# Attention and index heads taken in pairs, with the score products of two heads issued alternately

## The chip, the cores and the metric

The kernel runs on one core of one Trainium2 chip, as one program and one launch. The metric is device time in microseconds. The core's engines work side by side: TensorE (PE) multiplies matrices, VectorE (DVE) and ScalarE (ACT) work elementwise, SyncE (SP) issues the loads from HBM. Matrix products land in PSUM, which this kernel uses as 8 banks of 128 partitions x 2 KB.

## The reference

The reference is a network of three layers for one sequence of 256 tokens with 1024 features, in float32. Each layer takes a normalised and modulated input, mixes tokens, and has a feed-forward part. What matters here are the three mixing parts, in which every head has 64 features:

- First layer: 8 heads with a relative-position bias, beside a pooling branch and gates.
- Even layer: 8 heads with forget gates (a bias from cumulative sums), then 8 sliding-window heads with a sink and 2 shared key/value heads.
- Odd layer: 8 index heads score all pairs of tokens (`logits = einsum('bqhd,bsd->bqhs', iqi, ik)`, relu, weighted sum over heads); for each token the 64 best are kept; then 16 heads attend to those, with 4 shared key/value heads.

Each attention head computes softmax(q k^T + bias) v. The last feed-forward part is a mixture of 8 experts.

## The kernel before

Activations are kept as features x tokens, so a head's q and k are 64 partitions x 256 tokens. Two heads share a tile: one lies on partitions 0 to 63, the other on 64 to 127. The 256 query tokens are two blocks of 128, and the mask is causal, so a head's scores are a 128 x 128 product (first block) and a 128 x 256 product (second block), 384 columns in one PSUM bank. The products with weights (`mm3`, L212) are made in three passes of split float32r numbers; score products, transposes and value products are float32, which the chip runs as two passes each where an LDWEIGHTS and a MATMUL stand for one pass.

`attend` (L570) is a generator with five stages, one for each turn: (1) the two score products (`scores`, L562); (2) on DVE the sum with the bias and the row minimum (L580; scores are kept negated), on ACT the exponential with its row sum (L585), plus the sink's small steps in the sliding-window heads; (3) on DVE the reciprocal and the scaling (L595, L597); (4) on PE three transposes (L601), copied out of PSUM by ACT (L603); (5) for the second head of a pair, the value products of both heads, alternately, on the two halves of the output partitions (L610), and `after`, which splits the result into two float32r parts (L648, L649).

`weave` (L614) runs these generators. A turn advances every running head by one stage, oldest first, then starts one new head if its inputs are there, then does one step of a "piece": a quarter of a projection (`gemm_t_steps`, 12 matmul passes) or of an output product (`acc_steps`, 12 passes). So in steady state a head starts in each turn. A piece may wait for a number of finished heads: an output product needs its four heads. In the odd layer `weave` runs twice: first the 8 index heads (`index_head`, L1076: scores, then relu on ACT and weighted sums on DVE) and the selection (`select`, L1090, a chain of maxima and replacements on DVE), with three projections; then the 16 heads with two projections and three output products.

Two things set the order of work. The order of ACT's instructions is the order of the code (`ORDER = {'main': 'a', ...}`). The order on PE and DVE is planned by the framework from the data dependencies and its own estimate of times; it may, for example, put a score product between two transposes. Tiles come from rings: 8 PSUM banks for everything, 4 probability tiles (`N_PROB`), 3 transposed ones (`N_PROBT`), 2 bias tiles in the forget-gate heads, 8 small ones. While output products run, four banks hold their sums and one the sum of squares for the next norm (`acc_begin`, `norm_begin`).

Weights stream through `Stream` (L71): SP loads 5 tiles ahead, ACT and DVE split each into two parts (L195, L198), in the weaves by halves.

Of the kernel before, what the change touches and what calls it, by code (L numbers as in the profile page):

```python
# [152 lines left out]
class Kernel:  # L153
# [84 lines left out]
    def gemm_t_steps(self, key, h, kt, n=256, fine=False):  # L238
        """[n columns of w on partitions (two tiles a bank), tokens]"""
# [17 lines left out]
    def gemm_t2(self, keys, h):  # L257
        """Blocks of 256 columns, a row of h at a time as it is made"""
# [10 lines left out]
    def flush(self):  # L269
        """Work put off so that the tensor engine needn't wait for it"""  # L270
# [7 lines left out]
    def gemm_n_steps(self, key, h, fine=False):  # L278
        """[tokens on partitions (two tiles), 256 columns of w]"""
# [15 lines left out]
    def gemm_narrow(self, hi, lo, h):  # L295
        """[8 columns of w on partitions, tokens]"""
# [18 lines left out]
    def ada_step(self, layer, g, kt, raw, defer, weigh):  # L315
        """128 rows of a group of modulations' weights. weigh: on the vector engine, summed over the rows later"""
# [41 lines left out]
    def ada_turn(self, a):  # L358
        """The sums, on every 32nd partition, go to a column for each 128 of them"""
# [14 lines left out]
    def ada_finish(self, upto=None):  # L374
        """One step of what is left to do for the oldest group, or all that a group needs"""
# [19 lines left out]
    def rstd(self, ps, shape, first=None):  # L395
        """-2 / root of a mean square; the gains make up for the -2. first: a factor that goes ahead, in place"""
# [22 lines left out]
    def norm_begin(self, gain, layer=None, scale_i=None):  # L419
        """The norm that follows the coming updates of x"""  # L420
# [23 lines left out]
    def norm_first(self):  # L444
        """The first norm: the modulation is the last to come"""
# [89 lines left out]
    def acc_end(self, key, act, gate, n_ada):  # L535
        """The last rows: each feature tile goes on into the stream and its norm"""
# [33 lines left out]
    def attend(self, q, k, v, add, pair, sink=None, after=None):  # L570
        """One head, a stage at a time; a pair's second one ends both"""
        nc = self.nc
        ps = self.scores(self.psum(), q, k)
        if callable(add):
            add = add()
        yield
        p = self.sp.tile([128, 384], F32, name="prob", bufs=N_PROB)
        mn, sm = self.tiny(), self.tiny()
        for t, c in self.HALVES:
            nc.vector.tensor_tensor_reduce(out=p[:, c], in0=ps[:, c], in1=add[t], op0=OP.add, op1=OP.min,  # L580
                                           scale=1.0, scalar=3e38, accum_out=mn[:, t:t + 1])
        if sink is not None:
            nc.vector.tensor_scalar(mn, mn, sink, None, op0=OP.min)
        for t, c in self.HALVES:
            nc.scalar.activation(p[:, c], p[:, c], AF.Exp, bias=mn[:, t:t + 1], scale=-1.0,  # L585
                                 accum_out=sm[:, t:t + 1])
        if sink is not None:
            e = self.tiny()
            nc.vector.tensor_scalar(e, mn, sink, None, op0=OP.subtract)
            nc.scalar.activation(e, e, AF.Exp)  # L590
        yield
        if sink is not None:
            nc.vector.tensor_tensor(sm, sm, e, op=OP.add)
        ri = self.tiny()
        nc.vector.reciprocal(ri, sm)  # L595
        for t, c in self.HALVES:
            nc.vector.tensor_scalar(p[:, c], p[:, c], ri[:, t:t + 1], None, op0=OP.mult)  # L597
# [8 lines left out]
        if after:  # L606
            ps = self.psum()
            for t, (c, w) in enumerate(((0, 256), (128, 128))):
                for s, (vs, ps_t) in enumerate(pair):
                    nc.tensor.matmul(ps[64 * s:64 * s + 64, 0, c:c + w], vs[t], ps_t[:, 256 * t:256 * t + w],  # L610
                                     start=t == 0, stop=t == 1, skip_group_check=True)
            after(ps)

    def weave(self, heads, pieces):  # L614
        """Heads in a pipeline of stages, with the steps of other work between.
        heads: (pieces that have to be done, stages); pieces: (heads that have to be done, steps)"""
        running, h, p, done, piece = [], 0, 0, 0, None
        while h < len(heads) or p < len(pieces) or running:
            for g in list(running):
# [3 lines left out]
            if h < len(heads) and p >= heads[h][0]:  # L623
# [10 lines left out]
    def pair_out(self):  # L634
        """Where two heads' results meet, and their split for the product that follows"""
        nc = self.nc
        res, pairs = ([], []), {}

        def pair(j):
            return pairs.setdefault(j, [])  # L640
# [10 lines left out]
        return res, pair, after  # L651

# [128 lines left out]
    def layer1(self):  # L781
# [75 lines left out]
        att, pair, after = self.pair_out()  # L857
        heads = []
        for hd in range(8):
            def mk(hd=hd):  # L860
                j, s = hd // 2, hd % 2
                b = slice(64 * s, 64 * s + 64)
                bias = self.bias[j]
                return self.attend(qk[j // 2][b, j % 2], qk[2 + j // 2][b, j % 2],
                                   [vn[hd // 4][:, t, (hd % 4) * 64:(hd % 4) * 64 + 64] for t in range(2)],
                                   (bias[:, s, 128:256], bias[:, s, :]), pair(j), after=after(j) if s else None)
            heads.append((0 if hd < 4 else 4, mk))
# [72 lines left out]
    def even(self):  # L940
# [6 lines left out]
        # forget gates  # L947
# [53 lines left out]
        att, pair, after = self.pair_out()  # L1001
# [18 lines left out]
        for hd in range(8):  # L1020
            def mk(hd=hd):
                j, s = hd // 2, hd % 2
                b = slice(64 * s, 64 * s + 64)
                return self.attend(fq[j // 2][b, j % 2], fk[j // 2][b, j % 2],
                                   [fv[hd // 4][:, t, (hd % 4) * 64:(hd % 4) * 64 + 64] for t in range(2)],
                                   fox_bias(hd), pair(j), after=after(j) if s else None)
            heads.append((1 if hd < 4 else 3, mk))
        for j in range(4):
            for s in range(2):
                def mk(j=j, s=s):  # L1030
                    b = slice(64 * s, 64 * s + 64)
                    return self.attend(sq[j // 2][b, j % 2], self.sk[b, 0],
# [667 lines left out]
```

## Time and profile before

| what | value |
|---|---|
| median of 3 runs (lowest, highest) | 1365.48 us (1364.51, 1366.25) |
| span of the profiled execution | 1360.7 us |
| mean granted PE clock | 0.986 |
| TensorE busy | 1311.9 us (96%) |
| VectorE busy | 970.2 us (71%) |
| ScalarE busy | 737.6 us (54%) |
| DMA | 342.8 MB, mean 252 GB/s |

The span runs from the first to the last instruction on the core; the time of a run also holds what lies before and after. Busy times overlap between engines. Successive matmuls overlap in PE's pipeline, so the duration of one (0.28 us for a 256-column pass) is longer than the distance between two starts (0.12 us); prices on PE are read from starts. In a timeline, "x4" merges four neighbouring instructions of the same line, and fp32 products show two records each. Heads are at work from 63 to 111 us (first layer), 474 to 553 (even layer) and 810 to 898 (odd layer).

### The profile page before, as it was taken

How to read it: one execution, taken by the hardware profiler on the slowest of the kernel's cores; microseconds unless marked ns; L12 is line 12 of the kernel's file. 1: busy time of each engine (PE TensorE's matmuls, PEld its weight loads, DVE VectorE, ACT ScalarE, POOL GpSimd, SP SyncE). 2: the span in 40 equal slices, each digit the busy share in tenths (PEclk: the TensorE clock that was granted, in tenths of full speed). 3: DMA queues.
4: the chain of work that ended last, by engine and by line, in shares of the span. 5: the costliest groups of instructions: out<-in, count | busy, mean ns of one | idle time of the engine just before them, and what ended most of it. 6: DMA issues, size and time to landing. Idle time of an engine off the chain costs nothing. (4 is left out here: it accounts for less than half of the span.)

```text
span 1360.7 us, 22311 instructions
## 1 busy us (share of the span) xinstructions
PE 1311.9 (96%) x9230; PEld 1166.2 (86%) x9230; DVE 970.2 (71%) x1411; ACT 737.6 (54%) x928; POOL 4.1 (0%) x11
## 2 busy tenths in 40 slices
PE   5999999999999999999999999989999999999995
PEld 1777998899998887799999888669899899999994
DVE  3646865666567566666656579678889889889885
ACT  3645464544445454544334442656776776776773
POOL 0000000000000000000000000000000000000000
PEclk8899999999999999999999999999999999999997
DMA  9856947676664722577757553124998998997990
GB/s 370 333 194 245 407 188 274 232 284 233 266 226 188 302 97 76 192 300 301 279 216 278 193 225 109 48 93 177 351 355 293 350 374 283 341 371 276 348 374 34
DMA packets 54141, 342.81 MB, mean 252 GB/s; under 512 B 6061, under 2 KB 7349, under 8 KB 22928
## 3 DMA queue, kind: packets, MB, share of 16 engines
q1 hardware_dynamic: 53792, 341.02, 66.3%
q8 instruction: 74, 1.21, 0.4%
q0 software_dynamic: 240, 0.29, 0.2%
q14 instruction: 35, 0.29, 0.1%
HBM read 340.23 MB, written 1.06 MB: 251 GB/s over the span
## 5 line engine op out<-in xcount | busy, mean ns | idle before, releaser
L198 DVE TENSOR_TENSOR wlo<-raw,whi 128x2048 fp32r<-128x2048 f32 (+2 forms) x309 | 571.0, 1864 | 135.3 <-ACT whi L195 134.4
L195 ACT ACTIVATE whi<-raw 128x2048 fp32r<-128x2048 f32 (+2 forms) x309 | 482.7, 1573 | 181.8 <-PE ps L216 87.0
L214 PE MATMUL ps<-b,whi 128*128 128x256 f32 x1740 | 501.3, 289 | 1.2 <-ACT b L465 1.1
L215 PE MATMUL ps<-b,whi 128*128 128x256 f32 x1740 | 493.6, 284 | 0.5 <-DVE b L468 0.3
L216 PE MATMUL ps<-b,wlo 128*128 128x256 f32 x1740 | 493.1, 284 | 0.0
L214 PEld LDWEIGHTS ps<-b,whi 128*128 128x128 f32 x1740 | 333.7, 192 | 33.5 <-issue 16.1
L215 PEld LDWEIGHTS ps<-b,whi 128*128 128x128 f32 x1740 | 334.6, 192 | 3.2 <-issue 1.3
L216 PEld LDWEIGHTS ps<-b,wlo 128*128 128x128 f32 x1740 | 334.1, 192 | 1.8 <-issue 0.9
L215 PE MATMUL ps<-wlo,b 128*128 128x384 f32 (+2 forms) x800 | 267.0, 334 | 3.9 <-DVE wlo L198 3.9
L214 PE MATMUL ps<-whi,b 128*128 128x384 f32 (+2 forms) x800 | 267.0, 337 | 0.0
L216 PE MATMUL ps<-whi,b 128*128 128x384 f32 (+2 forms) x800 | 265.3, 332 | 0.0
L215 PEld LDWEIGHTS ps<-wlo,b 128*128 128x128 f32 x800 | 151.1, 189 | 13.7 <-DVE wlo L198 6.9
L214 PEld LDWEIGHTS ps<-whi,b 128*128 128x128 f32 x800 | 150.5, 189 | 9.0 <-issue 2.9
L216 PEld LDWEIGHTS ps<-whi,b 128*128 128x128 f32 x800 | 151.0, 189 | 7.3 <-issue 0.3
L344 PE MATMUL ps<-raw,cb 128*32 128x512 f32 x424 | 66.9, 639 | 14.3 <-DVE cb L672 9.4
L904 ACT ACTIVATE b<-ps,cols 128x256 f32<-128x256 f32 x44 | 24.7, 563 | 82.8 <-PE ps L216 53.5
L585 ACT ACTIVATE prob<-prob,tiny 128x128 f32<-128x128 f32 x80 | 35.7, 448 | 37.8 <-DVE tiny L580 20.7
L204 ACT ACTIVATE b<-b 128x512 fp32r<-128x512 f32 x24 | 15.2, 632 | 65.5 <-DVE b L929 44.6
L905 DVE SCALAR_TENSOR_TENSOR b<-ps,cols,b 128x255 f32<-128x255 f32 x44 | 21.2, 482 | 35.4 <-ACT b L904 35.3
L344 PEld LDWEIGHTS ps<-raw,cb 128*32 128x32 f32 x424 | 10.9, 111 | 38.9 <-DMA raw<-in_ada 13.5
L328 DVE SCALAR_TENSOR_TENSOR ada_acc<-raw,sc,ada_acc 128x2048 f32<-128x2048 f32 x16 | 37.5, 2347 | 4.6 <-DMA raw<-in_ada 4.5
L514 DVE SCALAR_TENSOR_TENSOR x<-ps,mod,x 128x256 f32<-128x256 f32 x72 | 31.1, 475 | 6.2 <-PE ps L216 5.8
(256 smaller groups left out, 977.8 us busy)
## 6 DMA issues: line engine op xcount, KB each, us to landing
raw<-in_ada SPq DMA_DIRECT2D x72, 1024.0 KB, 5.0
raw<-in_ed SPq DMA_DIRECT2D x40, 1024.0 KB, 7.7
raw<-in_eg SPq DMA_DIRECT2D x48, 768.0 KB, 5.6
raw<-in_eu SPq DMA_DIRECT2D x48, 768.0 KB, 5.5
raw<-in_w_up SPq DMA_DIRECT2D x22, 1024.0 KB, 5.5
raw<-in_w_in SPq DMA_DIRECT2D x16, 1024.0 KB, 7.0
raw<-in_w_down SPq DMA_DIRECT2D x11, 1024.0 KB, 6.8
raw<-in_e_fg SPq DMA_DIRECT2D x11, 1024.0 KB, 5.3
```

What stands on the lines that cost most here:

```text
L195: self.nc.scalar.activation(hi[:, c], raw[:, c], AF.Copy)
L198: self.nc.vector.tensor_tensor(lo[:, c], raw[:, c], hi[:, c].bitcast(F32), op=OP.subtract)
L204: nc.scalar.activation(hi, src, AF.Copy)
L214: mm(ps, ah, bh, start=start, stop=False, skip_group_check=True)
L215: mm(ps, ah, bl, start=False, stop=False, skip_group_check=True)
L216: mm(ps, al, bh, start=False, stop=stop, skip_group_check=True)
L328: nc.vector.scalar_tensor_tensor(a["acc"], raw, self.sc[:, c:c + 1], a["acc"], op0=OP.mult, op1=OP.add)
L344: self.nc.tensor.matmul(ps[32 * j:32 * j + 32, :], weights, rows[:, j * 512:(j + 1) * 512], start=start, stop=stop, skip_group_check=True)
L514: self.nc.vector.scalar_tensor_tensor(x, ps, gate[:, k:k + 1], x, op0=OP.mult, op1=OP.add)
L585: nc.scalar.activation(p[:, c], p[:, c], AF.Exp, bias=mn[:, t:t + 1], scale=-1.0, accum_out=sm[:, t:t + 1])
L904: nc.scalar.activation(y[:, j], ps[:, j], AF.Identity, scale=cw(2, j), bias=self.col("cb", base + j))
L905: nc.vector.scalar_tensor_tensor(y[:, j, 1:], ps[:, j, :T - 1], cw(1, j), y[:, j, 1:], op0=OP.mult, op1=OP.add)
```

## The change

`attend` takes two heads in place of one, `scores` makes both heads' products alternately (short, short, long, long), and each later stage loops over both. `weave` gets a turn counter: a pair may start when two turns (`every=2`) have passed since the last pair's start; in the index stage `every` is 1. The numbers of heads that pieces wait for are halved, except that the index stage's become 2, 3 and 4 pairs where they were 4, 6 and 8 heads. The value products are issued as before. Comments and docstrings go too, so line numbers shift.

```diff
-    def scores(self, ps, q, k):
-        ps = ps.rearrange("p a b -> p (a b)")
-        self.nc.tensor.matmul(ps[:, 0:128], q[:, 0:128], k[:, 0:128], start=True, stop=True)
-        self.nc.tensor.matmul(ps[:, 128:384], q[:, 128:256], k[:, 0:256], start=True, stop=True)
-        return ps
+    def scores(self, two):
+        pss = [self.psum().rearrange("p a b -> p (a b)") for _ in two]
+        for t, c in self.HALVES:
+            for ps, (q, k) in zip(pss, two):
+                self.nc.tensor.matmul(ps[:, c], q[:, t * 128:t * 128 + 128], k[:, 0:t * 128 + 128], start=True,
+                                      stop=True)
+        return pss
...
-    def attend(self, q, k, v, add, pair, sink=None, after=None):
+    def attend(self, two, after):
         nc = self.nc
-        ps = self.scores(self.psum(), q, k)
-        if callable(add):
-            add = add()
+        pss = self.scores([x[:2] for x in two])
+        adds = [x[3]() if callable(x[3]) else x[3] for x in two]
         yield
+        ps_, sums = [], []
+        for ps, add, (_, _, _, _, sink) in zip(pss, adds, two):
...
+        for p, (sm, e) in zip(ps_, sums):
...
-        pt = self.psum().rearrange("p a b -> p (a b)")
-        for i in range(3):
-            nc.tensor.transpose(pt[:, i * 128:i * 128 + 128], p[:, i * 128:i * 128 + 128], self.const("ident"))
-        pts = self.sp.tile([128, 384], F32, name="probt", bufs=N_PROBT)
-        nc.scalar.activation(pts, pt[:, 0:384], AF.Copy)
-        pair.append((v, pts))
+        pts = []
+        for p in ps_:
+            pt = self.psum().rearrange("p a b -> p (a b)")
+            for i in range(3):
+                nc.tensor.transpose(pt[:, i * 128:i * 128 + 128], p[:, i * 128:i * 128 + 128], self.const("ident"))
+            pts.append(self.sp.tile([128, 384], F32, name="probt", bufs=N_PROBT))
+            nc.scalar.activation(pts[-1], pt[:, 0:384], AF.Copy)
         yield
...
-    def weave(self, heads, pieces):
+    def weave(self, heads, pieces, every=2):
-        running, h, p, done, piece = [], 0, 0, 0, None
+        running, h, p, done, piece, turn, begun = [], 0, 0, 0, None, 0, -2
         while h < len(heads) or p < len(pieces) or running:
+            turn += 1
             for g in list(running):
                 if next(g, "end") == "end":
                     running.remove(g)
                     done += 1
-            if h < len(heads) and p >= heads[h][0]:
+            if h < len(heads) and p >= heads[h][0] and turn >= begun + every:
+                begun = turn
                 g = heads[h][1]()
...
-        pieces += [(4 * (i + 1), lambda i=i: out_piece(i)) for i in range(3)]
+        pieces += [(2 * (i + 1), lambda i=i: out_piece(i)) for i in range(3)]
...
-        heads = [(0, lambda hd=hd: index_head(hd)) for hd in range(8)]
+        heads = [(0, lambda j=j: index_heads(j)) for j in range(4)]
         heads += [(0, lambda t=t: select(t)) for t in range(2)]
-        self.weave(heads, [(4, k_piece), (6, lambda: q_piece(0)), (8, lambda: q_piece(1))])
+        self.weave(heads, [(2, k_piece), (3, lambda: q_piece(0)), (4, lambda: q_piece(1))], 1)
```

## Rows read from the trace of the kernel before

**Rows 1.** The page's first part: each engine's busy us, share, instructions.
```profile
PE 1311.9 (96%) x9230; PEld 1166.2 (86%) x9230; DVE 970.2 (71%) x1411; ACT 737.6 (54%) x928; POOL 4.1 (0%) x11
```
**Rows 2.** Stretches: start:end, length, busy us by engine, PE clock, DMA share, GB/s.
```profile
474.00:507.00 33.00, 33.00 (x230) 28.01 (x231) 20.55 (x70) 17.11 (x44) 0.00 (x0) 1.00 0.26 95
526.00:548.00 22.00, 21.84 (x138) 16.08 (x139) 14.98 (x70) 11.74 (x40) 0.00 (x0) 1.00 0.15 52
809.00:849.00 40.00, 39.70 (x290) 34.67 (x289) 35.28 (x98) 13.99 (x22) 0.00 (x0) 1.00 0.30 104
849.00:862.20 13.20, 12.28 (x61) 6.80 (x60) 10.86 (x48) 8.90 (x29) 0.00 (x0) 1.00 0.16 60
862.20:888.40 26.20, 26.20 (x185) 20.40 (x184) 15.80 (x66) 16.46 (x50) 0.00 (x0) 1.00 0.19 61
```
**Rows 3.** PE's waits in the odd layer: waiter, releaser, total us, times, longest.
```profile
PE ps L601 <- DVE prob L597: 0.9, 1, 0.9
```
**Rows 4.** Timeline of PE, first layer: start, us, line, operation, tiles, count.
```profile
65.45 0.28 PE L215 MATMUL ps<-b,whi 128*128 128x256 f32 x1
65.57 0.28 PE L216 MATMUL ps<-b,wlo 128*128 128x256 f32 x1
65.78 0.48 PE L564 MATMUL ps<-b 64*128 64x128 f32 x2
...
66.63 0.38 PE L214 MATMUL ps<-b,whi 128*128 128x256 f32 x1
66.85 0.28 PE L215 MATMUL ps<-b,whi 128*128 128x256 f32 x1
```
**Rows 5.** Timeline of PE, even layer: two sliding-window heads in a row.
```profile
528.06 0.50 PE L564 MATMUL ps<-b 64*128 64x128 f32 x4
...
528.92 0.39 PE L214 MATMUL ps<-b,whi 128*128 128x256 f32 x1
```
**Rows 6.** Timeline of PE: the first five index heads.
```profile
809.74 0.50 PE L564 MATMUL ps<-b 64*128 64x128 f32 x4 [0.30 <-DVE b L716]
...
810.50 0.49 PE L564 MATMUL ps<-b 64*128 64x128 f32 x4
...
811.15 0.38 PE L564 MATMUL ps<-b 64*128 64x128 f32 x2
811.37 0.59 PE L565 MATMUL ps<-b 64*128 64x256 f32 x2
811.90 0.39 PE L214 MATMUL ps<-b,whi 128*128 128x256 f32 x1
```
**Rows 7.** Timeline of PE, odd layer: a head between another head's transposes.
```profile
849.55 0.27 PE L601 MATMUL ps<-cst,prob 128*128 128x128 f32 x1
849.75 0.48 PE L564 MATMUL ps<-b 64*128 64x128 f32 x2
...
851.16 0.70 PE L715 MATMUL ps<-b,cst 128*128 128x512 f32 x1
```
**Rows 8.** Timeline of PE, odd layer: a head behind three transposes.
```profile
870.33 0.49 PE L601 MATMUL ps<-cst,prob 128*128 128x128 f32 x3
...
871.60 0.38 PE L214 MATMUL ps<-b,whi 128*128 128x256 f32 x1
```
**Rows 9.** Timeline of DVE: an index head's sum, the selection's last step.
```profile
820.00 0.75 DVE L1088 SCALAR_TENSOR_TENSOR score<-prob,iw,score 128x128 f32<-128x128 f32 x2 [1.73 <-ACT prob L1082]
...
847.30 0.43 DVE L1102 TENSOR_TENSOR sel<-sel,cst 128x256 f32<-128x256 f32 x1
```
**Rows 10.** Groups by line, 862.2 to 888.4: count, busy us, mean ns, idle before.
```profile
L585 ACT ACTIVATE prob<-prob,tiny 128x128 f32<-128x128 f32 (+1 forms) x17 | 7.5, 442 | 0.0
L580 DVE CUSTOM_DVE_ANT_0 prob<-ps,sel 128x256 f32<-128x256 f32 (+1 forms) x17 | 5.9, 348 | 0.0
L198 DVE TENSOR_TENSOR wlo<-raw,whi 128x1024 fp32r<-128x1024 f32 x4 | 4.9, 1221 | 0.0
L585 ACT ACTIVATION_READ_ACCUMULATOR prob<-prob,tiny 128x1 f32 x16 | 3.1, 191 | 0.0
```

More of the change, by code (lines that the diff above doesn't have):

```diff
@@ L568 @@
     HALVES = ((0, slice(0, 128)), (1, slice(128, 384)))
-    def attend(self, q, k, v, add, pair, sink=None, after=None):
+    def attend(self, two, after):
         nc = self.nc
-        ps = self.scores(self.psum(), q, k)
-        if callable(add):
-            add = add()
+        pss = self.scores([x[:2] for x in two])
+        adds = [x[3]() if callable(x[3]) else x[3] for x in two]
         yield
[L577 to L590, printed above, removed]
-        yield
[L592 to L597, printed above, removed]
-        yield
-        pt = self.psum().rearrange("p a b -> p (a b)")
-        for i in range(3):
-            nc.tensor.transpose(pt[:, i * 128:i * 128 + 128], p[:, i * 128:i * 128 + 128], self.const("ident"))
-        pts = self.sp.tile([128, 384], F32, name="probt", bufs=N_PROBT)
-        nc.scalar.activation(pts, pt[:, 0:384], AF.Copy)
-        pair.append((v, pts))
-        yield
[L606 to L612, printed above, removed]
@@ L614, in weave @@
-    def weave(self, heads, pieces):
-        running, h, p, done, piece = [], 0, 0, 0, None
+        ps_, sums = [], []
+        for ps, add, (_, _, _, _, sink) in zip(pss, adds, two):
+            p = self.sp.tile([128, 384], F32, name="prob", bufs=N_PROB)
+            mn, sm = self.tiny(), self.tiny()
+            for t, c in self.HALVES:
+                nc.vector.tensor_tensor_reduce(out=p[:, c], in0=ps[:, c], in1=add[t], op0=OP.add, op1=OP.min,
+                                               scale=1.0, scalar=3e38, accum_out=mn[:, t:t + 1])
+            if sink is not None:
+                nc.vector.tensor_scalar(mn, mn, sink, None, op0=OP.min)
+            for t, c in self.HALVES:
+                nc.scalar.activation(p[:, c], p[:, c], AF.Exp, bias=mn[:, t:t + 1], scale=-1.0,
+                                     accum_out=sm[:, t:t + 1])
+            e = None
+            if sink is not None:
+                e = self.tiny()
+                nc.vector.tensor_scalar(e, mn, sink, None, op0=OP.subtract)
+                nc.scalar.activation(e, e, AF.Exp)
+            ps_.append(p)
+            sums.append((sm, e))
@@ new lines, in attend @@
+        yield
+        for p, (sm, e) in zip(ps_, sums):
+            if e is not None:
+                nc.vector.tensor_tensor(sm, sm, e, op=OP.add)
+            ri = self.tiny()
+            nc.vector.reciprocal(ri, sm)
+            for t, c in self.HALVES:
+                nc.vector.tensor_scalar(p[:, c], p[:, c], ri[:, t:t + 1], None, op0=OP.mult)
+        yield
+        pts = []
[5 more added lines that the diff above has]
+            nc.scalar.activation(pts[-1], pt[:, 0:384], AF.Copy)
@@ L618, in weave @@
+        yield
+        ps = self.psum()
+        for t, (c, w) in enumerate(((0, 256), (128, 128))):
+            for s in range(2):
+                nc.tensor.matmul(ps[64 * s:64 * s + 64, 0, c:c + w], two[s][2][t], pts[s][:, 256 * t:256 * t + w],
+                                 start=t == 0, stop=t == 1, skip_group_check=True)
+        after(ps)
+    def weave(self, heads, pieces, every=2):
+        running, h, p, done, piece, turn, begun = [], 0, 0, 0, None, 0, -2
         while h < len(heads) or p < len(pieces) or running:
+            turn += 1
@@ L636, in pair_out @@
         nc = self.nc
-        res, pairs = ([], []), {}
-        def pair(j):
-            return pairs.setdefault(j, [])
+        res = ([], [])
         def after(j):
@@ L650, in after @@
             return f
-        return res, pair, after
+        return res, after
     def setup(self):
@@ L856, in layer1, with mk, head @@
         self.fgl_w, self.iw_w, self.rw_w = (self.narrow_weight(name) for name in ("e_fgl", "o_iw", "rw"))
-        att, pair, after = self.pair_out()
+        att, after = self.pair_out()
         heads = []
[L859 to L867, printed above, removed]
+        for j in range(4):
+            def mk(j=j):
+                def head(s):
+                    b, hd, bias = slice(64 * s, 64 * s + 64), 2 * j + s, self.bias[j]
+                    return (qk[j // 2][b, j % 2], qk[2 + j // 2][b, j % 2],
+                            [vn[hd // 4][:, t, (hd % 4) * 64:(hd % 4) * 64 + 64] for t in range(2)],
+                            (bias[:, s, 128:256], bias[:, s, :]), None)
+                return self.attend([head(s) for s in range(2)], after(j))
+            heads.append((0 if j < 2 else 4, mk))
         pieces = [lambda: qk_piece(1), lambda: qk_piece(3), lambda: v_piece(1), lambda: p_piece(0),
@@ L999, in sq_piece @@
             sq[i] = self.rope((yield from self.gemm_t_steps(("e_in", 6 + i), h, 8, fine=FINE))[0], q=True)
-        att, pair, after = self.pair_out()
+        att, after = self.pair_out()
         def fox_bias(hd):
@@ L1019, in even, with mk, head @@
         heads = []
[L1020 to L1027, printed above, removed]
-        for j in range(4):
-            for s in range(2):
-                def mk(j=j, s=s):
-                    b = slice(64 * s, 64 * s + 64)
-                    return self.attend(sq[j // 2][b, j % 2], self.sk[b, 0],
-                                       [self.sv[:, t * 128 + 64 * s:t * 128 + 64 * s + 64] for t in range(2)],
-                                       (mw[:, 128:256], mw), pair(4 + j), after=after(4 + j) if s else None,
-                                       sink=self.nsink[:, 4 * s + j:4 * s + j + 1])
-                heads.append((6 if j < 2 else 7, mk))
+        for j in range(4):
+            def mk(j=j):
+                def head(s):
+                    b, hd = slice(64 * s, 64 * s + 64), 2 * j + s
+                    return (fq[j // 2][b, j % 2], fk[j // 2][b, j % 2],
+                            [fv[hd // 4][:, t, (hd % 4) * 64:(hd % 4) * 64 + 64] for t in range(2)],
+                            fox_bias(hd), None)
+                return self.attend([head(s) for s in range(2)], after(j))
+            heads.append((1 if j < 2 else 3, mk))
+        for j in range(4):
+            def mk(j=j):
+                def head(s):
+                    b = slice(64 * s, 64 * s + 64)
+                    return (sq[j // 2][b, j % 2], self.sk[b, 0],
+                            [self.sv[:, t * 128 + 64 * s:t * 128 + 64 * s + 64] for t in range(2)],
+                            (mw[:, 128:256], mw), self.nsink[:, 4 * s + j:4 * s + j + 1])
+                return self.attend([head(s) for s in range(2)], after(4 + j))
+            heads.append((6 if j < 2 else 7, mk))
         def flush():
@@ L1074, in odd, with index_heads @@
         mc = self.const("mc")
-        def index_head(hd):
-            b = slice(64 * (hd % 2), 64 * (hd % 2) + 64)
-            j = hd // 2
-            ps = self.scores(self.psum(), iq[j // 2][b, j % 2], ik[b, 0])
+        def index_heads(j):
+            bs = [slice(64 * s, 64 * s + 64) for s in range(2)]
+            pss = self.scores([(iq[j // 2][b, j % 2], ik[b, 0]) for b in bs])
             yield
-            r = self.sp.tile([128, 384], F32, name="prob", bufs=N_PROB)
-            nc.scalar.activation(r, ps[:, 0:384], AF.Relu)
-            for t, c in self.HALVES:
-                w = iw[:, t * 8 + hd:t * 8 + hd + 1]
-                if hd == 0:
-                    nc.vector.tensor_scalar(score[:, c], r[:, c], w, None, op0=OP.mult)
-                else:
-                    nc.vector.scalar_tensor_tensor(score[:, c], r[:, c], w, score[:, c], op0=OP.mult, op1=OP.add)
+            for s, ps in enumerate(pss):
+                hd = 2 * j + s
+                r = self.sp.tile([128, 384], F32, name="prob", bufs=N_PROB)
+                nc.scalar.activation(r, ps[:, 0:384], AF.Relu)
+                for t, c in self.HALVES:
+                    w = iw[:, t * 8 + hd:t * 8 + hd + 1]
+                    if hd == 0:
+                        nc.vector.tensor_scalar(score[:, c], r[:, c], w, None, op0=OP.mult)
+                    else:
+                        nc.vector.scalar_tensor_tensor(score[:, c], r[:, c], w, score[:, c], op0=OP.mult, op1=OP.add)
         def select(t):
@@ L1136, in odd @@
         pieces = [(0, lambda: q_piece(2)), (0, lambda: q_piece(3)), (0, flush)]
-        pieces += [(4 * (i + 1), lambda i=i: out_piece(i)) for i in range(3)]
+        pieces += [(2 * (i + 1), lambda i=i: out_piece(i)) for i in range(3)]
         self.weave(heads, pieces)
@@ L1535 @@
 N_PROB = 4
-N_PROBT = 3
+N_PROBT = 4
 N_FILL = 5
```

18 lines of the change are left out of this document (9 added, 9 removed).

## Prediction

> **What bounds the kernel now.** I read the engines' totals first: TensorE (PE) is busy for 1311.9 of 1360.7 us, and no other engine comes near [rows 1]. That figure is an average, so I then took the busy times of the stretches in which heads are worked on. In the forget-gate heads (474 to 507) and in the second half of the odd layer (862.2 to 888.4) PE is busy for the whole stretch; from 526 to 548 and from 809 to 849 it misses 0.16 and 0.30 us, and only from 849 to 862.2 does it lack 0.92 us [rows 2]. Where PE never waits, an instruction taken out of its queue comes off the span at its full length. The exception is 849 to 862.2: no projection step is left to run there, VectorE (DVE) is busy for 10.86 of 13.20 us, and the one long wait of PE is for DVE's scaled probabilities [rows 2, 3]. That stretch is a chain, not a queue of PE.
>
> **What a head's scores cost on PE.** A head's two score products are four PE passes, two each (x2 at L564). The timeline prices them in place. Projection passes start every 0.12 us (65.45, 65.57). With one head between them the next two start at 66.63 and 66.85. From 65.57 to 66.85 is 1.28 us; two passes would have taken 0.24, so a lone head costs 1.04 us. Only part of this is streaming: entering costs 0.21 instead of 0.12, and the second projection pass behind it comes after 0.22 instead of 0.12 [rows 4].
>
> What two adjacent heads on opposite partition halves cost is already in this trace. At 528.06 a second head happened to be issued right behind the first: both short products together (x4), then the long ones, and the next projection starts at 528.92. That is 0.86 us for two heads, against 0.85 (65.78 to 66.63) for one [rows 4, 5]. So a pair costs 1.04 + 0.01 = 1.05 us, and the second head is free.
>
> One rule speaks for less. The Trainium skill (TensorE: Matmul & The Clock Gate, "The mechanism") says that matmuls start and end strictly in issue order, and that only different row groups overlap. The change alternates products, and each product is two passes on its own half, so under strict order a second pass would hold up the other head's first. From the lone head's passes (0.11 us short, 0.22 long [rows 6]) I work out an estimate of 0.88 us of streaming instead of 0.66, some 0.2 us more per pair, or 4 us less gain over 20 pairs. The trace does not bear this out: at 528.06 the code issues the whole first head before the second, and the second's short product still starts before the first's long one [rows 5]. I go by the row.
>
> **The sum.** Going along the timeline from 63.34 to 887.59, I find 48 heads in these groups: 32 alone; 7 cut in two by transposes that were planned between the short and the long product; 2 neighbouring pairs; and the first 5 index heads back to back.
> - Alone: 32 x 1.04 = 33.3 us.
> - Cut in two: three transposes and the head take 849.55 to 851.16 = 1.61 us, against 870.33 to 871.60 = 1.27 uncut [rows 7, 8]. So each costs 1.04 + 0.34 = 1.38; seven are 9.7 us.
> - Pairs: 2 x 1.05 = 2.1 us.
> - The five: 809.74 to 811.90 = 2.16, plus 0.19 for entering and leaving = 2.35 us [rows 6].
>
> Together 47.4 us. Afterwards there are 20 attention pairs (4 first layer, 8 even, 8 odd) at 1.05 = 21.0 us. The index heads become four pairs. The loop takes one new pair a turn and lets the first projection begin when two are done, so three stand together and the fourth comes behind a projection step: 0.76 + 0.65 (the pair-to-pair distances at 809.74, 810.50, 811.15) + 0.86 + 0.19 = 2.46, plus 1.05, is 3.5 us. Together 24.5. On PE alone the change takes out 22.9 us.
>
> **What does not come through.** From 849 to 862.2, five heads (one alone, four cut) cost PE 6.6 us and would cost 2.6, which is 4.0 of the 22.9. But PE is not the limit there. The first output product needs four heads finished, and these wait for the selection mask, which DVE finishes at 847.73 [rows 9]. Two things still shorten the chain: the index heads are done sooner (DVE idled 1.73 us before the last one at 820.00 [rows 9]), and fewer heads' softmaxes lie on DVE between the mask and that product. I credit 1.5 us of the 4.0 and take off 2.5; the bounds are nothing credited (4.0 off) and all of it (0 off).
>
> The pairs also make the work burstier, and PSUM has 8 banks. From the first output product on, four accumulators and the norm's sum hold five. A pair wants two banks for scores, later two for its transposes and one for its result, so its second transposed head has to wait until DVE has read the next pair's first scores (about two L580, 0.70 us [rows 10]). Nine pairs run in that state (four sliding-window, five in the odd layer). A projection step of 12 passes (1.44 us) lies between these scores and the transposes and hides the 0.70 while DVE is free. DVE is busy for 15.80 and ScalarE (ACT) for 16.46 of 26.2 us in that stretch; four pairs at 1.03 less would leave about 22.1 us, 72 and 74% [rows 2]. I take 0.15 us per pair, 1.4 in all; the bounds are 0 (as now, with PE never waiting) and the whole 0.70 each, 6.3.
>
> The softmax of two heads is one chain now. ACT takes four exponentials and four accumulator reads (4 x 0.44 + 4 x 0.19 = 2.5 us); a first L580, the reciprocal and the scaling of the last head add about 1.2, and queueing behind one weight split another 1.2, so 4.9 us, an estimate [rows 10]. Pairs begin every second turn, so between a pair's scores and its transposes PE has three steps (4.3 us), the previous pair's transposes (0.5) and a value product (0.9): 5.7 us of cover. If a second split or copy held the chain by more than 0.8 us, the transposes would be late by the excess. Nothing else is added: the value products were already issued for two heads together, and the exponentials, copies and weight loads are the same in number. DMA moves 52 to 104 GB/s in these stretches [rows 2], so weights do not become the limit, and the feed-forward and expert stages only start earlier.
>
> Sum: 22.9 - 2.5 - 1.4 = 19.0 us off. The profiled span of 1360.7 becomes 1341.7. The median of the runs shown, 1365.5, lies 4.8 above that span, time around the first and last instruction that the change does not touch, so the prediction is **1346.5 us**.
>
> **The rivals.**
> - *Half is given back as waits.* PE gets faster than the softmax chain can follow: if each of the 20 pairs' transposes comes 0.5 us late, 10 us return, about 1356. For it: ACT runs in program order, so the exponentials stand behind the copies of the pair before, and its spare time shrinks. Against it: 5.7 us of cover for 4.9.
> - *The pairs do not stay together.* PE's order is planned, not written; the planner has cut seven heads already (one of them in [rows 7]). If it moved one head of each pair away, only the cuts and the index stage would gain, some 4 us: 1361. Against it: both heads' inputs are ready at the same time, and two heads that were ready together did stay together [rows 5].
> - *Slower.* The PSUM shortage decides: from the first output product, a pair's transposes wait for banks that DVE frees only after the next pair's whole softmax input and the weight split before it. The nine pairs would have to lose over 2.2 us each (19.0 + 1.4 over 9) before the change costs time; at 2.6 us each (four L580 and a weight split of 1.22 [rows 10]) it comes to 1368.5. The Trainium skill warns of just this (TensorEngine Tiling (Array Packing), "Gotcha 1: PSUM Pressure": row tiling raises the pressure on the banks). Against it: the present order also wants up to four banks of three there, and PE does not wait [rows 2].
>
> **How the numbers follow.** The forecast with its own range of 1341 to 1351 (all cover holds, or the bounds of the chain and the bank waits) has 0.64. Half given back, 1351 to 1359, has 0.22; pairs apart, 1359 to 1363, 0.05; slower 0.06; 0.03 is left for other ways to end within 0.2%. The range 1341 to 1355 leaves out about 2 in 10. A measurement of this kernel tells about 0.2%, 2.7 us, from no change. Faster by more: 0.89; within: 0.05; slower by more: 0.06.
>
> **What would show it.** In the new trace there should be some 22 groups of score passes, each under 0.9 us from the first to the next other pass, and the two heads' short products should start within a few hundredths of a microsecond. The distance between pairs in the late odd stretch should fall from 6.55 (26.2 / 4) to about 5.5 us. PE's idle time before transposes there should stay under 0.3 us a pair, and the stretch without projections should shrink by less than PE's work in it. I am wrong if PE shows waits for DVE or ACT in front of transposes or scores that add up to over 5 us, or if score groups of one head remain.

## The result and the profile after

The changed kernel takes 1343.18 us (median of 4 runs, 1341.66 to 1343.83); the kernel before took 1364.99 beside it (4 runs, 1362.18 to 1366.25). The ratio is 0.984, with a 95% interval of 0.983 to 0.986. Forecast were 1346.5 us and a range of 1341 to 1355. The span of the profiled execution went from 1360.7 to 1341.3 us, 19.4 less; the forecast was 19.0. The medians are 21.8 us apart, because the profiled execution of the kernel before was one of its shorter ones (its runs in this record lie between 1361.7 and 1367.0 us).

Two things about the change itself. It also raises the ring of transposed tiles (`N_PROBT`) from 3 to 4, which the section on the change leaves out. ACT's copies into that ring waited, in the kernel before, for nothing but the transposes (L601), so the profile shows no limit in three tiles there; whether pairs would do with three was not run. And the numbers that the index stage's pieces wait for are halved like the others.

PE's total on the page answers [rows 1]: 23.1 us less work on PE, while VectorE (DVE) is where it was.

```profile
PE 1288.8 (96%) x9230; PEld 1154.0 (86%) x9230; DVE 971.4 (72%) x1411; ACT 734.8 (55%) x928; POOL 4.1 (0%) x11
```

PE's timeline after, first layer, answers [rows 4]. All eight records of a pair stand as one group (x8). From its first product to the next projection pass it is 0.86 us (67.77 to 68.63), as [rows 5] had it for two heads and [rows 4] for one.

```profile
67.56 0.28 PE L216 MATMUL ps<-b,wlo 128*128 128x256 f32 x1
67.77 0.93 PE L568 MATMUL ps<-b 64*128 64x128 f32 x8
68.63 0.38 PE L214 MATMUL ps<-b,whi 128*128 128x256 f32 x1
68.85 0.28 PE L215 MATMUL ps<-b,whi 128*128 128x256 f32 x1
...
862.68 0.93 PE L568 MATMUL ps<-b 64*128 64x128 f32 x8
...
868.04 0.93 PE L568 MATMUL ps<-b 64*128 64x128 f32 x8
```

There are 22 such groups in the whole trace, 21 pairs and one of three index pairs; 20 of the pairs take 0.85 to 0.86 us and the very first 0.94. In the late odd layer a pair now comes every 5.36 us (862.68 to 868.04), where two heads took 6.55.

Stretches of the trace after, columns as in [rows 2]. The first has the same projection passes in it as 847.16 to 862.83 of the kernel before (15.67 us, of which PE lacked 0.92), the second runs to the scores of the last attention pair. In the first PE lacks 2.23 us, and DVE is busy for 12.06 of 13.13. In the second PE is busy throughout.

```profile
835.11:848.24 13.13, 10.90 (x78) 7.38 (x76) 12.06 (x53) 9.33 (x32) 0.00 (x0) 1.00 0.17 61
848.24:868.90 20.66, 20.66 (x180) 17.54 (x179) 16.04 (x63) 15.49 (x49) 0.00 (x0) 1.00 0.24 78
```

PE's waits after (columns as in [rows 3]). The transposes' wait for the scaled probabilities grew from 0.9 to 2.1 us in total [rows 3]; the wait for L997, in front of a transpose of the even layer's shared value, has no row in the answer for the kernel before.

```profile
PE ps L612 <- DVE prob L606: 2.1, 2, 1.9
...
PE ps L1001 <- ACT b L997: 1.2, 1, 1.2
```

To see where the 19.4 us come from, I gave every start-to-start distance on PE to the line of the first of the two instructions, idle time apart, and compared the sums of both traces between the first and the last projection pass:

| PE time, before minus after | us |
|---|---|
| scores (L564, L565 to L568) | +18.1 |
| transposes of probabilities | +3.7 |
| value products | +1.8 |
| projections, rotations, norms | +0.7 |
| modulation products (L344) | -1.5 |
| pooling products (L824 to L832) | -0.4 |
| idle time | -3.3 |
| all else | +0.1 |
| sum | 19.2 |

The first three rows go with the pairs. Idle time and modulation take 4.8 us back: 1.3 of the idle time in the stretch from 835.11, 1.0 in the even layer (the wait for L997).

The modulation was not foreseen in the sum. A modulation batch is four products on four column groups (32 columns each) which run side by side: four take 1.00 us (118.44 to 119.44 in the kernel before, below), and one alone takes 0.98. PE's order is planned anew for every kernel, and in the changed one the planner pulled three batches of the first layer apart. PE's timeline after, each part a batch of its own (x2 is one product, x6 three):

```profile
111.27 1.05 PE L344 MATMUL ps<-raw,cb 128*32 128x512 f32 x2
112.25 0.97 PE L832 MATMUL ps<-b 128*128 128x256 f32 x6
113.14 1.06 PE L344 MATMUL ps<-raw,cb 128*32 128x512 f32 x6
114.13 0.39 PE L214 MATMUL ps<-b,whi 128*128 128x256 f32 x1
...
115.04 1.04 PE L344 MATMUL ps<-raw,cb 128*32 128x512 f32 x2
116.01 0.38 PE L214 MATMUL ps<-b,whi 128*128 128x256 f32 x1
116.33 1.06 PE L344 MATMUL ps<-raw,cb 128*32 128x512 f32 x6
117.31 0.39 PE L214 MATMUL ps<-b,whi 128*128 128x256 f32 x1
...
178.97 1.04 PE L344 MATMUL ps<-ada_acc,ones 128*32 128x512 f32 x2
...
185.41 1.06 PE L344 MATMUL ps<-ada_acc,ones 128*32 128x512 f32 x6
```

One product holds PE for 0.98 us (111.27 to 112.25, 115.04 to 116.01), and so do three (0.99 from 113.14 to 114.13). The kernel before had cuts too, but others; its timeline in the same part of the layer:

```profile
113.74 1.90 PE L344 MATMUL ps<-raw,cb 128*32 128x512 f32 x10
...
118.44 1.06 PE L344 MATMUL ps<-raw,cb 128*32 128x512 f32 x8
119.44 0.39 PE L214 MATMUL ps<-b,whi 128*128 128x256 f32 x1
...
181.20 1.07 PE L344 MATMUL ps<-ada_acc,ones 128*32 128x512 f32 x8
```

At the projection pass that the kernel before starts at 111.80 us the changed kernel is ahead by 3.36 us, at the one it starts at 227.43 by only 0.52. So 2.8 us were given back between the two (2.9 in the expectations below), and modulation has 2.3 of them.

### The profile page after: what moved, and what is told of

Its sections match the earlier page's. It is cut to its first block, busy times and chain, and to the rows that moved or that the text cites. A ratio compares the mean times of both kernels' runs of the same rounds, so it can differ in the third digit from the quotient of the medians.

```text
span 1341.3 us, 22321 instructions
## 1 busy us (share of the span) xinstructions
PE 1288.8 (96%) x9230; PEld 1154.0 (86%) x9230; DVE 971.4 (72%) x1411; ACT 734.8 (55%) x928; POOL 4.1 (0%) x11
## 5 line engine op out<-in xcount | busy, mean ns | idle before, releaser
L344 PE MATMUL ps<-raw,cb 128*32 128x512 f32 x424 | 67.3, 636 | 14.8 <-DVE cb L680 9.6
L344 PEld LDWEIGHTS ps<-raw,cb 128*32 128x32 f32 x424 | 10.5, 110 | 39.1 <-DMA raw<-in_ada 14.7
```

Of the source, the lines that this page charges most:

```text
L344: self.nc.tensor.matmul(ps[32 * j:32 * j + 32, :], weights, rows[:, j * 512:(j + 1) * 512], start=start, stop=stop, skip_group_check=True)
```

## The experiments

Theory: the gain is the second head's streaming that now lies beside the first's, plus fewer changes between narrow and full-width products; what is missing was given back by the planner's cuts and by the chain through DVE. Rivals: the alternate issue matters; the gain is only the grouping; the given-back time is something else; PSUM is nearly short.

**The yardstick.** The changed kernel on the chip of the next three.

> The changed kernel once more, as the yardstick of the three kernels beside it on the same chip. Every theory: about 1343 us, 21 to 22 us below the kernel before (0.984 of it).

1343.53 us, ratio 0.984 (0.983 to 0.986): the time expected, 20.5 us below the kernel before (1364.00 on this chip) where 21 to 22 were expected. From 60 us to the end of the heads the same instructions keep their distance to the first trace within 0.1 us but for one stage, told at the end.

**Is it the alternate issue?**

```diff
-        for t, c in self.HALVES:
-            for ps, (q, k) in zip(pss, two):
+        for ps, (q, k) in zip(pss, two):
+            for t, c in self.HALVES:
```

> The changed kernel with the two loops of a pair's score products exchanged: first head's short and long product, then the second head's, still next to each other on TensorE and still on the two halves of the rows. Theory (the halves run beside each other by themselves, as the one pair in the rows of before did; the alternate issue adds nothing): each pair still takes 0.85 us from its first product to the next instruction, the time is that of the changed kernel within 0.3%, 1341 to 1346 us. Rival (products start strictly in the order of issue, so that a second long product of one half holds up the other half): the second head's short product starts only when the first head's long one does, each pair takes about 0.2 us longer, 24 pairs 4 to 5 us, 1347 to 1349 us.

1342.77 us, ratio 0.984 (0.982 to 0.985). The same pair in PE's timeline, issued head after head:

```profile
66.73 0.93 PE L568 MATMUL ps<-b 64*128 64x128 f32 x8
67.59 0.38 PE L214 MATMUL ps<-b,whi 128*128 128x256 f32 x1
```

Again 0.86 us. In PE's planned order the first head's two products do stand ahead of the second's here, and yet in the records the second head's short product starts 13 ns after the first's (7 ns in the alternate order). The rival with strict order falls: it is enough that the two heads stand next to each other, and the order within the pair is free.

**Is it the two halves?** The second head is scored with the first head's q and k, so both stand on one half.

```diff
-            for ps, (q, k) in zip(pss, two):
+            for ps, (q, k) in zip(pss, two[:1] * 2):
```

> The changed kernel, in which the second head of each pair is scored with the first head's q and k, so that both stand on the same half of the partitions (the second head's scores are therefore the first head's). Issue order, groups, softmax and all else are as in the changed kernel. Theory (the gain is that the two halves run beside each other): the second head's two products, 0.11 + 0.22 us per pass and two passes, no longer lie beside the first's: about 0.64 us more for each of 24 pairs, 15 us, 1356 to 1361 us; the distance from a group's first product to the next instruction goes from 0.85 to about 1.5 us. Rival (the gain is from the order: fewer groups, fewer changes between narrow and wide products): the groups take some 0.85 to 1.0 us as well, 1342 to 1347 us.

1353.73 us, ratio 0.994 (0.992 to 0.996). The pair in PE's timeline:

```profile
67.59 1.57 PE L568 MATMUL ps<-b 64*128 64x128 f32 x8
69.09 0.39 PE L214 MATMUL ps<-b,whi 128*128 128x256 f32 x1
```

1.50 us, 0.65 more than on two halves; scores cost 15.5 us more over the trace. The theory's price of the overlap holds, but the time rose by 10 to 11 us only (the trace by 10.5) and missed the 1356 to 1361 expected. With the pairs slower, the long wait for L606 (1.91 us at 838.14 in the changed kernel) is gone and the stretch around it is 1.3 us shorter, where its own scores make it 1.3 longer. That is 2.6 of the some 4.5 us that are missing; the rest lies in smaller places. The rival holds a share as well: this kernel still beats the one before by 0.6%. So the 1.03 us that a pair saves (2 x 1.04 less 1.05) is 0.65 for overlap and 0.38 for one entry and exit in place of two.

**What do the cut modulation batches cost?** First all of them put together:

```diff
-        for j in range(4):
-            self.nc.tensor.matmul(ps[32 * j:32 * j + 32, :], weights, rows[:, j * 512:(j + 1) * 512], ...
+        with self.tc.high_priority():
+            for j in range(4):
+                self.nc.tensor.matmul(ps[32 * j:32 * j + 32, :], weights, rows[:, j * 512:(j + 1) * 512], ...
```

> The changed kernel, with the four column-group products of each modulation step (L344) at high priority, so that the four stand together in TensorE's order (75 batches planned instead of 85); a few groups of scores and value products are cut into 3 and 1 in exchange. Theory (the 2.9 us given back in the first layer are modulation batches that were cut, at about 1.05 us for each extra batch): ten batches fewer give up to 10 us, less some 0.3 to 0.5 us for each newly cut group of heads, 1334 to 1341 us, and the records show L344 in fours. Rival (the give-back comes from loads or from the order of other work, the cuts run beside it): no gain, 1342 to 1346 us.

1360.75 us, ratio 0.998 (0.997 to 0.999): 17 us slower than the changed kernel, a plain miss. The batches did become whole and PE spends 10.5 us less on them, as priced. But they moved earlier, away from waits that they had filled. PE's waits in this kernel have one line that in the changed kernel was 3.1 us in 2:

```profile
PE ps L214 <- ACT b L510: 14.8, 6, 2.9
```

One of them in PE's timeline, and then two stretches behind it (columns as in [rows 2]; the granted clock is the third figure from the end, 0.55 in the first and 1.00 in the second):

```profile
226.83 1.13 PE L474 MATMUL ps<-b,ones_d 128*128 128x256 f32 x4
230.88 0.50 PE L214 MATMUL ps<-b,whi 128*128 128x256 f32 x2 [2.92 <-ACT b L510]
231.53 0.38 PE L215 MATMUL ps<-b,whi 128*128 128x256 f32 x1
231.75 0.28 PE L216 MATMUL ps<-b,wlo 128*128 128x256 f32 x1
```

```profile
231.53:235.20 3.67, 3.67 (x18) 3.67 (x19) 3.67 (x8) 1.91 (x5) 0.00 (x0) 0.55 1.01 426
235.50:239.00 3.50, 3.50 (x30) 2.53 (x29) 0.88 (x2) 3.47 (x4) 0.00 (x0) 1.00 0.32 133
```

In the changed kernel the same place, between the norm's sum (L473) and the next projection, is full of modulation:

```profile
221.74 1.13 PE L473 MATMUL ps<-b,ones_d 128*128 128x256 f32 x4
222.80 2.78 PE L344 MATMUL ps<-raw,cb 128*32 128x512 f32 x24
225.93 1.05 PE L344 MATMUL ps<-raw,cb 128*32 128x512 f32 x2 [0.35 <-DMA raw<-in_ada]
226.91 0.39 PE L214 MATMUL ps<-b,whi 128*128 128x256 f32 x1
```

Four such waits of 2.9 us stand open that the changed kernel does not show (230.88, 453.43, 580.17, 789.36), and idle time grows by 17.8 us in all. The projections cost 7.5 us more besides, with not one more of them: behind three of the four (not behind the one at 789.36, where it is 1.00) the granted clock falls to near its lower level of 1.2 GHz, with 18 passes in 3.67 us against 30 in 3.50.

The same edit on the kernel before:

> The kernel before with the same high priority on the modulation products (75 batches planned instead of 84), to see what the edit is worth without the pairs. Theory (a cut batch costs 1.05 us wherever it stands): 5 to 9 us below the kernel before, 1356 to 1360 us. Rival (cuts are hidden by waits for the modulation weights): the same as the kernel before within 0.2%. If this edit gains as much here as on the changed kernel, the give-back was not the pairs' own cost but where the order fell.

1378.29 us, ratio 1.010 (1.008 to 1.012): 14 us slower, for the same reason (PE waits for L510 for 13.5 us in 5). Both expectations fall; the edit costs much the same without the pairs, 14 us against 17, so the pairs are not its cause.

**Only the batches that fill no wait.** First the three extra ones of the changed kernel's first layer (and one that they displace), then four more. A batch is named by its group of modulations and its step in the group, both counted from 0.

```diff
-        for j in range(4):
...
+        if start:
+            self.ada_n = getattr(self, "ada_n", -1) + 1
+            a["n"] = [self.ada_n, -1]
+        a["n"][1] += 1
+        with self.tc.high_priority() if tuple(a["n"]) in ((1, 4), (1, 5), (1, 6), (2, 0)) else nullcontext():
+            for j in range(4):
...
```

> The changed kernel, with high priority for the products (L344) of four modulation batches of the first layer alone: those that stood cut there in the records of the changed kernel (near 111 to 116 and 179 to 185 us). TensorE's planned order then has 82 batches in place of 85; scores, value products and everything after 190 us stand as before. Putting all batches together was 17 us slower, since batches that had stood in four waits of the normalisation (2.9 us each) had moved away from them. Theory (the 2.9 us given back in the first layer are the extra batches themselves, about 1.05 us each, and these stood in no wait): 3 us below the changed kernel, 1339 to 1341 us, and the passes after 190 us start some 3 us earlier. Rival (these too filled waits, or the give-back comes from elsewhere): no gain, 1342 to 1345 us, and new idle time in the first layer.

1340.23 us (1339.96 to 1341.23), ratio 0.983 (0.981 to 0.984), against 1343.53 for the changed kernel on the other chip. The two intervals overlap and the kernel before took 1.3 us less on this chip, so the times alone would not settle it; the trace does. PE spends 3.3 us less on modulation, and the passes from 186.40 on start 3.65 us earlier (there at 182.75). The batch near 115 us is whole, with 0.33 us of wait behind it:

```profile
115.22 1.06 PE L349 MATMUL ps<-raw,cb 128*32 128x512 f32 x8
116.62 0.50 PE L214 MATMUL ps<-b,whi 128*128 128x256 f32 x2 [0.33 <-ACT b L204]
```

> As the kernel with four batches whole, with three more that are cut in the kernel before as well (near 220 to 260 us): 79 batches planned in place of 85, the rest of the order unchanged. Theory (each extra batch outside a wait costs 1.05 us): 6 us below the changed kernel, 1336 to 1338.5 us. Rival (extra batches are free, something covers them): 1342 to 1345 us. Third (those near 230 us stand in the wait of the normalisation that the high-priority kernel laid open): 3 us gained and up to 2.9 us lost with a lower clock behind it, 1339 to 1343 us.

1337.0 us (1335.98 to 1338.19), ratio 0.980 (0.979 to 0.982); on another chip 1337.26, ratio 0.981 (0.979 to 0.982). The set in the diff is (1, 4) to (1, 7), (2, 0), (3, 0), (3, 5) and (3, 7). The theory holds: modulation costs 6.6 us less, and about 6.3 us come out. This version beats both kernels.

> The changed kernel with eight modulation batches whole once more, as the yardstick on the same chip: 1336 to 1338 us by every theory.

> The kernel before with the same modulation batches whole as in the kernel with eight whole, and the one more that is cut in it (79 batches planned in place of 84; scores and all other order as in the kernel before). It puts both kernels on the same number of batches. Theory (the 2.9 us given back in the first layer are only where the batches fell, not a price of the pairs): five batches fewer, 5 us, 1358 to 1360 us, so that the pairs are then worth 21 to 23 us between this kernel and the one with eight batches whole. Rival (the batches of the kernel before filled waits of its own, so that the extra ones were free): 1362 to 1365 us.

1361.09 us, ratio 0.999 (0.998 to 1.000), beside 1337.26 for the changed kernel with its batches whole. Neither theory nor rival: modulation costs 5.1 us less, as priced, but only some 2 us come out (2.3 against the kernel before on the same chip), and 4.7 us of idle time are new. Of these, 1.4 lie ahead of the heads, at 50.87, and the pass behind them starts only 0.1 us later than in the kernel before. PE's waits in that kernel name one of the other places:

```profile
PE ps L214 <- ACT b L204: 1.4, 1, 1.4
```

This wait can't be the whole cause: the changed kernel with eight batches whole has it too (1.33 us at 117.62) and gains all the same. Why five batches gave back so little here stays open.

At equal numbers of batches the pairs are worth 1361.1 - 1337.3 = 23.8 us. The 2.8 us given back could be won back with the pairs left as they are, so they were a price of the planner's cuts and not of the pairs. But neither is a cut batch a fixed price: three fewer gave 3.3 us, six 6.3, five in the kernel before 2, and ten -17.

**How near is PSUM to short?**

```diff
-        return self.pp.tile([128, 2, 256], F32, name="ps", bufs=8)
+        return self.pp.tile([128, 2, 256], F32, name="ps", bufs=7)
```

> The changed kernel with seven PSUM tiles in place of eight. The prediction took off 1.4 us for waits on PSUM tiles (nine pairs of the odd layer, 0.15 us each); the trace of the changed kernel shows none there. Theory (PSUM has room to spare in the odd layer, and the missing waits are not luck): less than 2 us slower, 1342 to 1345 us, and no idle time before the transposes (L612) in the pairs of the odd layer. Rival (the eight tiles only just suffice, as the prediction had it): each of nine pairs there waits for the softmax chain of the pair before, 0.5 us or more, 1348 us or above.

1344.18 us, ratio 0.985 (0.984 to 0.987): the theory's time, but not its absence of waits. PE's waits and one of the places in its timeline:

```profile
PE ps L612 <- DVE prob L606: 2.2, 3, 1.8
...
PE ps L612 <- DVE tiny L585: 0.5, 2, 0.2
```

```profile
860.95 0.49 PE L612 MATMUL ps<-cst,prob 128*128 128x128 f32 x3
861.67 0.55 PE L612 MATMUL ps<-cst,prob 128*128 128x128 f32 x3 [0.23 <-DVE tiny L585]
861.98 0.36 PE L214 MATMUL ps<-b,whi 128*128 128x256 f32 x1
```

This is the wait that the prediction named (the second head's transposes wait until DVE has read the next pair's scores), but it appears with one bank fewer, in two places, at 0.23 us. Split in this way, the two transpose groups let the passes behind them start some 0.4 us later each time.

**Pairs at a faster pace.**

```diff
-    def weave(self, heads, pieces, every=2):
+    def weave(self, heads, pieces, every=1):
```

> The changed kernel, in which the weave of heads and projection pieces begins a pair at every turn in place of every second one. A pair of the odd layer takes TensorE some 3.0 us without the pieces (1.3 for scores, 0.8 for the transposes, 1.0 for the value products), VectorE 2.0 us and ScalarE 1.9 us of its own softmax work and 0.4 to 0.5 us more each of copies. Theory (projection pieces between the pairs are what covers the softmax chain; with pairs at half the distance the chain, 3 to 4 us from score to transpose, lies open and PSUM tiles are held by more pairs at once): idle time before the transposes (L612) of 0.5 to 2 us per pair in the odd layer, 1345 to 1360 us. Rival (chain and PSUM have room to spare at that pace too): 1341 to 1345 us, no idle time there.

1343.61 us, ratio 0.985 (0.984 to 0.987): the changed kernel's time. Some pairs of the odd layer now come 3.14 us apart (848.36 and 851.50), and PE's waits for probabilities are shorter, not longer (2.1 in the changed kernel):

```profile
PE ps L612 <- DVE prob L606: 1.1, 2, 0.9
```

The theory falls: no idle time of 0.5 to 2 us per pair appears, so chain and PSUM have room at that pace as well, though a wait of 0.84 us for a copied transpose is new (L619 at 530.65). The equal time is in part luck: transposes and value products cost PE 2.2 and 2.0 us more than in the changed kernel, and projections, modulation and the rest some 4 us less.

## Why the prediction was right, and where not

*Bound and price of a pair: right.* The pairs measure what [rows 4] and [rows 5] said. The two parts that make it up were not separated there; the same-half kernel did that. Forecast were 22.9 us on PE; scores and transposes gave 21.8. That PE's total fell by 23.1 is nearer than the working deserves: it also holds 1.8 of value products, which the old order had cut three times and the new one keeps whole, and it is net of 1.5 more modulation.

*The row against the rule: the row was right.* The Trainium skill (TensorE: Matmul & The Clock Gate, "The mechanism") has matmuls start strictly in issue order, which by the prediction's estimate makes a pair some 0.2 us dearer. The traces disagree: 0.86 us in both orders, and where the heads are issued one after the other, the second head's short product still starts ahead of the first's long one (66.740 and 67.052 us).

*The odd layer's chain: right in kind, too dear.* I took off 2.5 us where PE waits for DVE; the idle time there grew by 1.3. The stretch became 2.5 us shorter (15.67 to 13.13), where 1.5 had been credited.

*PSUM waits: wrong place, one bank too early.* I took off 1.4 us; the stretch from 848.24 shows none.

*Not in the sum:* 1.5 us more modulation, from the planner's cuts, and 1.0 us for L997. The rival of pairs drawn apart had named the planner, but for the wrong instructions: the pairs stayed together, and it was products that the change does not touch which it cut.

*The step that failed* is the last one: the "time around the first and last instruction" of 4.8 us. I set the profiled span against the median of other executions. The profiled execution of the changed kernel has 1343.05 us to a span of 1341.3, and a run of the kernel before has 1362.54 to 1360.8: 1.7 us lie around the span (1.7 to 1.9 in every run of the kernel before whose span is listed). The runs of the kernel before lie between 1361.7 and 1367.0 us, and the profiled execution was at the lower end; the rest of the 4.8 is that spread. What makes its longer runs long is not shown. With 1.7 the same sum gives 1343.4; measured were 1343.2. The other errors (-1.1 scores and transposes, +1.8 value products, +1.2 chain, +1.4 PSUM, -1.5 modulation, -1.0 L997, and smaller ones) cancel to 0.4 us in the span, which is luck.

*The sign of being wrong* was set too low. It was waits of over 5 us for DVE or ACT in front of transposes or scores. With the changed kernel these come to 4.9 us for the heads (2.1 before transposes, 2.8 before scores), and to 6.1 with the transpose that waits for L997. But 3.7 stood in the kernel before already (0.9 and 2.8), which the sign did not count; the growth is 1.2, or 2.4.

*Rivals.* "Half is given back" by late transposes: these cost 1.2 us, not 10. "Slower" by PSUM: no wait of the kind with eight banks, two of 0.23 us with seven.

## What to carry to other kernels

Price an edit to a packed engine queue by start-to-start distances in the trace; where a neighbouring case is already there by accident, it is worth more than a rule. When the order is planned, compare every line's share of the queue after an edit, not only the lines that were edited: products that run side by side cost their whole price for each part that they are cut into (here about 1 us), and putting them together did not pay where they had filled waits. Take the time around the span from an execution whose time and span are both known.

## What the runs showed of the hardware

A wait can cost more than its length. In the kernel with all batches whole, PE idled 2.92 us at 230.88 and then ran at a granted clock of 0.55 (18 passes in 3.67 us), near its lower level of 1.2 GHz. The 1.91 us wait of the changed kernel (0.92 in the kernel before) can do the same: in its first trace the clock behind it is 1.00, but in the trace of the kernel with four batches whole the same wait, at 834.26, is followed by this:

```profile
834.26:838.00 3.74, 3.61 (x18) 3.34 (x19) 2.97 (x13) 3.42 (x12) 0.00 (x0) 0.65 0.05 8
```

In the second trace of the changed kernel the clock falls there too, and that stage takes 1.08 us longer than in the first:

```profile
839.00:843.00 4.00, 4.00 (x23) 2.98 (x22) 3.05 (x10) 2.39 (x10) 0.00 (x0) 0.75 0.42 121
```

It is the one stage of the heads in which its two traces differ by more than 0.1 us. Eight traces of kernels with pairs have this wait at 1.74 to 1.92 us. In five the granted clock of the 4 us behind it is 0.58 to 0.76, in three it is 1.00; the changed kernel and the one with eight batches whole have one trace of each kind. Why it falls in some executions and not in others stayed open. The wait that the pairs lengthened in the odd layer thus costs 1.9 us, and in the second trace 1.1 us more.
